# A two-layer encoder on one core: first-layer tokens grouped by residue modulo 16, and the third group's probabilities turned by VectorE

## The chip, the cores and the metric

The kernel runs on one core of one Trainium2 chip. A core has five engines, each with an instruction queue of its own: TensorE (PE; its weight loads are listed apart as PEld), VectorE (DVE), ScalarE (ACT), GpSimd (POOL) and SyncE (SP, which here only issues DMA transfers). PE writes its products to PSUM, in banks of 512 floats per partition; everything else lies in SBUF, 128 partitions wide, or in DRAM. The metric is the device time of one execution in microseconds. The kernel before takes 941.91 us, the median of three runs (941.63 to 941.92).

## The reference

An encoder of two layers on 512 tokens of 1024 features. The first layer's mixer is attention in three groups per head, and this is the part that the change touches; the second layer uses grouped-query attention over all tokens. Every layer has memory attention (4 heads, 256 memory tokens), a SiLU gate and an output projection.

```python
A_GROUPS = ((128, 1), (512, 4), (2048, 16))      # (window, dilation)

def mixer_dilated(qkv, qn_g, kn_g, ang):         # qkv: 3 x 3 groups x 8 heads x 128
    ...
    q = apply_rope(rmsnorm(q), ang) * (HEAD_DIM ** -0.5)
    k = apply_rope(rmsnorm(k), ang)
    for g, (window, dilation) in enumerate(A_GROUPS):
        # token t attends to t + j*dilation, |j| <= window/(2*dilation)
        o_g, l_g = dilated_window_attention(q[:, :, g], k[:, :, g], v[:, :, g], window, dilation)
    w = softmax over the three groups of their log-sum-exps
    return sum over g of w_g * o_g

for i in range(2):
    h = rmsnorm(x, norm_g[i])
    proj = h @ w_in[i]                           # mixer heads, memory queries, gates
    ...
    y = concatenate([o_mix, o_mem]) * silu(gate)
    x = x + y @ w_out[i]
```

With 512 tokens, the second group joins tokens of one residue class modulo 4 (128 of them, all within its window's blocks of 128 up to a mask), and the third one tokens of one residue class modulo 16 (32 of them).

## The kernel before

**Weights and products.** The weights (1024 rows, four bytes a number) stream from DRAM in transfers of 512 KB, issued by SP and in part by GpSimd (L261). Each large product is made from seven products of sums of blocks (named "12", "11", "S1", "S2", "S4", "S3", "22"; of both factors). For precision each factor is a rounded high part and a low part, its remainder: the weights' high part is cast by ScalarE (L323), the low part is subtracted by DVE (L333), and PE takes three products of parts, L176, L177 and, for the weights' low parts, L180. The partial results in PSUM (pool `pj`, four banks) are copied out by ScalarE (L398) or added onto a tile `sn` by DVE (L420). Transposes, scores and attention products use a second pool of four banks (`at`).

**Tokens.** Chunk c (0 to 3) of the first layer holds the tokens 4p+c, p = 0 to 127 on the partitions. The transposed rows of x have the chunks side by side, p along the free dimension; products of the projection again have p on the partitions. One chunk is thus a residue class modulo 4: the second group attends inside a chunk, and the third one inside the tokens with equal p modulo 4 of a chunk. `first_t` and `diffs_t` transpose the normed rows on PE into a PSUM bank and read them from there; `setup` loads the mask and the rotary table `tabA` with p on the partitions, and the weights `grA` of the norms.

**One head** (`head_chunk`, then `attn_a`). A chunk of the projection gives q, k and v of the three groups for one head. After norm and rotation q and k are transposed (L641); `put` (L1255 to L1263) copies them: `qs`, `ks` for groups two and three with columns in order of the chunk, and `qk0` for the first group with columns in token order, written with a step of four floats. v of groups two and three stays in place (`v12`). v of the first group, of all heads, was computed before and stored in DRAM in token order (`v0d`, by `ev_v0`, L1183, eight transfers).

In `attn_a`, o = 0 is the first group, with probabilities of 128 tokens by 256 neighbours; o = 1 the second and the third together, 128 by 2 x 128 per chunk. The scores (L1298, L1302) get the mask and their maximum on DVE (L1308) and the exponential on ScalarE (L1280). The statistics (maximum and sum) are swapped between the two orders of tokens through DRAM: tile `ds`, stored by L1336 and L1337, loaded back by L1339 and L1340 (SP). From them come factors for each token, by which `scale` (L1376, head 7 L1374) multiplies the probabilities. `turn(1)` transposes eight 128x128 blocks on PE (L1389) into two banks, the first copied by ScalarE, the second by DVE (L1393, `copy`); k = 0 is the second group, k = 1 the third. `turn(0)` does the same for the first group. `pv` multiplies by v (L1410 for o = 1), and `comb` adds the first group's result to that of the others (L1422). The head's output, 128 features by 512 tokens in order of the chunks, goes to DRAM (`od`), but for head 7.

**The gates** (`gates`, used for both layers). Three chunks "m", "a" and "b" project the gates, transposed (features on the partitions, tokens along the free dimension). Each result gets tanh (ScalarE) and (1 + tanh) times itself (DVE); then `times` multiplies by the head's output, loaded back as `og` from `od` (L862) or, where a head's output is still in SBUF, one head at a time (L866). What comes out, `y` in high and low parts (L890, L892) or sums of it, is the moving factor of the output projection, whose result is added to x and goes to the second layer with tokens p on the partitions.

**Order.** The schedule is written out by hand. A driver hands out slots: between groups of PE's matmuls it runs one step of each generator; each `yield n` waits n slots; `drv.late`, `drv.soon` and `drv.spawn` put work into queues for later slots. Chunks of the first layer run in the order "01234567mab": while PE multiplies for chunk h, attention of head h-1 is interleaved, so heads 6 and 7 fall beside the gate chunks. Each engine runs its own queue strictly in that order.

## Time and profile before

| | before |
|---|---|
| time, median of 3 runs | 941.91 us (941.63 to 941.92) |
| the profiled execution: its time | 942.24 us |
| the profiled execution: span of the trace | 940.5 us |
| granted clock of TensorE over the span | 1.00 |
| HBM read, written | 158.31 MB, 11.08 MB |

The span runs from the first recorded instruction to the last; the execution's own time has 1.7 us around it. Rows give, for a group of instructions, the line of the kernel, the engine, the operation, the tile written and those read, shapes and count, then busy time, the mean of one in ns, and the idle time of that engine just before them with what ended it. The costliest groups:

```profile
L333 DVE TENSOR_TENSOR wo<-wl,wh 128x1024 fp32r<-128x1024 f32 x258 | 316.4, 1232 | 7.0 <-ACT wh L323 6.8
L323 ACT CAST wh<-wl 128x1024 fp32r<-128x1024 f32 x258 | 271.7, 1060 | 29.7 <-PE pj L177 15.6
L176 PE MATMUL pj<-wh,hS 128*128 128x512 f32 (+1 forms) x416 | 154.3, 380 | 0.0
```

The low parts of the weights take 316.4 us of DVE, the high parts 271.7 us of ScalarE.

### The profile page before, as it was taken

The page shows a single profiled execution, that of the slowest core. Times are in us where ns is not written, and L with a number is a line of the kernel's source. Part 1 is how long each engine was busy: PE and PEld are TensorE (multiplying, and loading weights), DVE is VectorE, ACT ScalarE, POOL GpSimd, SP SyncE. Part 2 cuts the span into 40 slices and gives each one's busy share as a digit, 9 for nine tenths or more (in the row PEclk, how much of TensorE's full clock was granted, in tenths as well). Part 3 has the DMA queues.
Part 4 walks back from the last instruction along what each step waited for, and adds up shares of the span by engine and source line. Part 5 has one row for each costly group of instructions (what it writes and reads, how often), then busy time and mean ns, then how long its engine had stood idle before and what let it go on. Part 6 is the DMA issues. An engine that isn't in the chain of part 4 may idle for free.

```text
span 940.5 us, 16300 instructions
## 1 busy us (share of the span) xinstructions
PE 932.8 (99%) x5500; PEld 819.9 (87%) x5500; DVE 798.6 (85%) x1442; ACT 691.3 (74%) x1720; POOL 346.0 (37%) x494
## 2 busy tenths in 40 slices
PE   8999999999999999999999999999999999999998
PEld 6889888888888888888889998888988999999886
DVE  6898676879888888889788899977998998689977
ACT  7775788677768686867675667637878887789774
POOL 3411425455554545463836111114262440111123
PEclk9999999999999999999999999999999999999999
DMA  9999937869787878696867889979985686785777
GB/s 355 386 259 336 299 91 190 278 139 256 158 250 147 260 154 268 158 268 136 249 165 206 246 200 243 305 229 326 270 203 122 166 239 168 199 221 126 190 173 179
DMA packets 89429, 207.15 MB, mean 220 GB/s; under 512 B 25217, under 2 KB 34689, under 8 KB 89346
## 3 DMA queue, kind: packets, MB, share of 16 engines
q1 hardware_dynamic: 68818, 140.64, 43.4%
q0 software_dynamic: 19520, 63.97, 36.9%
q10 hardware_dynamic: 1008, 1.51, 0.4%
q8 instruction: 43, 0.70, 0.3%
q14 instruction: 40, 0.33, 0.1%
HBM read 158.31 MB, written 11.08 MB: 180 GB/s over the span
## 4 chain that ended last, share of the span: by engine, by line
PE 91%; DVE 4%; DMA 3%; ACT 1%; issue 0%; SPq 0%; DVEq 0%; ACTq 0%
PE pj L176 24%; PE pj L177 24%; PE pj L180 23%; PE qT L641 2%; DMA og<-od 2%; PE ptb L1616 1%; PE sa L1302 1%; PE oo L1410 1%; PE pt L1389 1%; DMA wl<-in_wall_dram 1%; PE xT L536 1%; PE sa L1298 1%; DVE wo L333 1%; PE ob L180 1%; PE ob L177 1%; PE ob L176 1%
## 5 line engine op out<-in xcount | busy, mean ns | idle before, releaser
L333 DVE TENSOR_TENSOR wo<-wl,wh 128x1024 fp32r<-128x1024 f32 x258 | 316.4, 1232 | 7.0 <-ACT wh L323 6.8
L323 ACT CAST wh<-wl 128x1024 fp32r<-128x1024 f32 x258 | 271.7, 1060 | 29.7 <-PE pj L177 15.6
L176 PE MATMUL pj<-wh,hS 128*128 128x512 f32 (+1 forms) x416 | 154.3, 380 | 0.0
L177 PE MATMUL pj<-wh,hS 128*128 128x512 f32 (+1 forms) x416 | 148.9, 367 | 0.0
L176 PE MATMUL pj<-wh,h 128*128 128x512 f32 (+1 forms) x312 | 115.2, 378 | 0.0
L177 PE MATMUL pj<-wh,h 128*128 128x512 f32 (+1 forms) x312 | 111.7, 367 | 0.0
L484 POOL TENSOR_TENSOR rstd<-mse,half 128x4 f32<-128x4 f32 (+2 forms) x98 | 103.0, 1051 | 8.2
L180 PE MATMUL pj<-wo,hS 128*128 128x512 f32 (+1 forms) x416 | 99.5, 366 | 0.0
L177 PEld LDWEIGHTS pj<-wh,hS 128*128 128x128 f32 x416 | 78.7, 189 | 11.3
L176 PEld LDWEIGHTS pj<-wh,hS 128*128 128x128 f32 x416 | 78.6, 189 | 11.1 <-DVE sn L420 0.2
L483 POOL TENSOR_SCALAR mse<-hss 128x4 f32<-128x4 f32 (+1 forms) x88 | 46.1, 524 | 103.2 <-ACT junk L629 95.5
L180 PEld LDWEIGHTS pj<-wo,hS 128*128 128x128 f32 x416 | 72.4, 189 | 13.1
L629 ACT ACTIVATE junk<-sn 128x128 f32<-128x128 f32 x264 | 79.3, 311 | 2.2 <-DVE sn L411 2.1
L1246 POOL TENSOR_TENSOR ta<-sn,tabs 128x128 f32<-128x128 f32 (+1 forms) x64 | 35.9, 567 | 120.1 <-DVE sn L634 92.8
L398 ACT COPY sn<-pj 128x512 f32<-128x512 f32 x122 | 67.2, 590 | 16.6 <-PE pj L180 15.8
L180 PE MATMUL pj<-wo,h 128*128 128x512 f32 (+1 forms) x312 | 74.5, 365 | 0.0
L307 POOL DMA_DIRECT2D wl<-wl x34 | 30.2, 898 | 114.8 <-DVE wo L333 74.6
L261 POOL DMA_DIRECT2D wl<-in_wall_dram x40 | 38.1, 968 | 81.6 <-DMA wl<-in_wall_dram 35.3
L420 DVE TENSOR_TENSOR sn<-pj,sn 128x512 f32<-128x512 f32 x89 | 60.8, 684 | 7.1 <-PE pj L180 6.6
L177 PEld LDWEIGHTS pj<-wh,h 128*128 128x128 f32 x312 | 59.0, 189 | 8.4
L176 PEld LDWEIGHTS pj<-wh,h 128*128 128x128 f32 x312 | 59.0, 189 | 8.2
L180 PEld LDWEIGHTS pj<-wo,h 128*128 128x128 f32 x312 | 54.3, 189 | 9.7
(283 smaller groups left out, 2366.7 us busy)
## 6 DMA issues: line engine op xcount, KB each, us to landing
wl<-in_wall_dram SPq DMA_DIRECT2D x224, 512.0 KB, 7.5
wl<-wl POOLq DMA_DIRECT2D x68, 512.0 KB, 5.5
wl<-in_wall_dram POOLq DMA_DIRECT2D x44, 512.0 KB, 8.3
od<-o SPq DMA_DIRECT2D x11, 256.0 KB, 5.1
og<-od SPq DMA_DIRECT2D x10, 256.0 KB, 9.8
x<-in_x_dram SPq DMA_DIRECT2D x4, 512.0 KB, 9.0
v0d<-sn SPq DMA_DIRECT2D x8, 256.0 KB, 10.5
acc<-in_x_dram POOLq DMA_DIRECT2D x8, 256.0 KB, 7.1
```

The source lines that it names most:

```text
L176: T.matmul(o, a, b, start=start, stop=False, skip_group_check=True)
L177: T.matmul(o, c, d, start=False, stop=False, skip_group_check=True)
L180: T.matmul(o, a, b, start=False, stop=stop, skip_group_check=True)
L261: queue.dma_start(t, wall[d], **how)
L323: A.copy(wh, self.tile[self.items[i]])
L333: V.tensor_tensor(wo, self.tile[key], wh.bitcast(F32), ALU.subtract)
L398: A.copy(t, b)
L420: V.tensor_tensor(t, b, t, ALU.subtract if q == "12" else ALU.add)
L483: G.tensor_scalar(e, ss, EPS, None, ALU.add)
L484: G.tensor_tensor(r, e, half[:, 0:n], ALU.pow)
L629: A.activation(jk, p[:, j * 128:(j + 1) * 128], AF.Square, scale=by, accum_out=ss[:, j:j + 1])
L1246: G.tensor_tensor(ta[:, 0:n], xn[:, 0:n, 0:32], ropeA[:, 0, b, s0:s0 + n], ALU.mult)
```

## The change

Inside each chunk of the first layer the tokens get another order: column i*32 + a holds p = 4a + i (i = 0 to 3, a = 0 to 31), so that a residue class modulo 16 is a block of 32 columns. The order is made where the transposed rows of x are read from PSUM (`from_rows` on the read side, `by_class` on the written side); the products of the projection then have it on their partitions. The third group's probabilities of a chunk are now zero outside four diagonal blocks of 32x32, so the transpose of the 128x128 tile is that of its 32x32 blocks, and one `V.transpose` for the head takes the place of four PE transposes and of DVE's copy of their bank. The rest follows the order: the mask's half for groups two and three and the rotary table are loaded with the partitions in the new order (the mask through a tile `ok` and two GpSimd copies that also reorder its columns), v of the first group is stored in four transfers of 32 partitions instead of one, the copies into `qk0` write with a step of 16 floats instead of 4, `comb` reads with that step, the statistics' tile `ds` is laid out with the owner outermost, and the gates of the first layer (`perm=True`) write their product back in order of p, with a step of four floats, where their second tile `th` takes it in chunk "b". The second layer's calls are unchanged (`same`).

```diff
+    def by_class(t):
+        return t.rearrange("p k (i a) -> p k i a", i=4)
-    def first_t(H, top, c):
-        ps = [(k, turn4(top[j], *slot(H, k, c))) for k, j in (("12", 1), ("11", 0))]
-        for k, p in ps:
-            A.copy(whole(k, c), p)
+    def first_t(H, top, c, view=same, turn=same):
+        ps = [(k, turn(turn4(top[j], None, None)), [view(t) for t in slot(H, k, c)]) for k, j in (("12", 1), ("11", 0))]
+        for k, p, hl in ps:
+            split(*hl, p)
+        for k, p, _ in ps:
+            A.copy(view(whole(k, c)), p)
...
-    def gates(od, o_done, o_here, direct, forms=False):
+    def gates(od, o_done, o_here, direct, forms=False, perm=False):
...
+                def cls(t):
+                    return t.rearrange("p (m i a) -> p m i a", i=4, a=32) if perm else t
+                def rws(t):
+                    return t.rearrange("p (m a i) -> p m i a", i=4, a=32) if perm else t
...
-                        V.tensor_tensor(dst, t, got["o"], ALU.mult)
+                        V.tensor_tensor(rws(dst), cls(t), cls(got["o"]), ALU.mult)
...
-                            V.tensor_tensor(dv[:, n], tv[:, n], got[h][:, n], ALU.mult)
+                            V.tensor_tensor(rws(dv[:, n]), cls(tv[:, n]), cls(got[h][:, n]), ALU.mult)
...
-                times(t)
+                y = th if perm else t
+                times(y)
...
+    def from_rows(p):
+        return p.rearrange("p k (a i) -> p k i a", i=4)
...
     def setup():
-        nc.sync.dma_start(mask, mask_d)
-        nc.sync.dma_start(tabA, tab_a.rearrange("p (b c d) -> p b c d", b=2, c=4))
+        nc.sync.dma_start(mask[:, 0:256], mask_d[:, 0:256])
+        ok = s2(name="ok")[:, 0:256]
+        nc.sync.dma_start(ok, mask_d[:, 256:512].rearrange("(a i) k -> i a k", i=4))
+        nc.sync.dma_start(tabA.rearrange("p b c d -> p (b c d)"), tab_a.rearrange("(a i) f -> i a f", i=4))
...
+        for g in range(2):
+            G.tensor_copy(mask[:, 256 + g * 128:384 + g * 128].rearrange("p (i a) -> p i a", i=4), ok[:, g * 128:(g + 1) * 128].rearrange("p (a i) -> p i a", i=4))
...
-    v0w = v0d.rearrange("(p c) d -> c p d", c=4)
+    v0w = v0d.rearrange("(a i c) d -> c i a d", i=4, c=4)
...
-        nc.sync.dma_start(v0w[2 * i + u][:, j * 512:(j + 1) * 512], t)
+        for c in range(4):
+            nc.sync.dma_start(v0w[2 * i + u][c, :, j * 512:(j + 1) * 512], t[32 * c:32 * c + 32])
...
-                    A.copy(qk0[:, 0].rearrange("p (a c) -> p c a", c=4)[:, b], p[:, 0])
-                    V.tensor_scalar(qk0[:, 1].rearrange("p (a c) -> p c a", c=4)[:, b], p[:, 3], gk[:, 0:1], None, ALU.mult)
+                    q0, k0 = [qk0[:, n].rearrange("p (a i c) -> p c i a", i=4, c=4)[:, b] for n in range(2)]
+                    A.copy(q0, p[:, 0].rearrange("p (i a) -> p i a", i=4))
+                    V.tensor_scalar(k0, p[:, 3].rearrange("p (i a) -> p i a", i=4), gk[:, 0:1], None, ALU.mult)
...
-        ds = dram.tile([S, 2, 2], F32, name="ds")
-        nat_v = ds.rearrange("(b p) o s -> p b o s", b=4)
-        str_v = ds.rearrange("(p b) o s -> p b o s", b=4)
+        ds = dram.tile([2, S, 2], F32, name="ds")
+        nat_v = ds.rearrange("o (b p) s -> o p b s", b=4)
+        str_v = ds.rearrange("o (a i b) s -> o i a (b s)", i=4, b=4)
...
-                parts = [[(b, k) for b in range(4)] for k in range(2)]
+                parts = [[(b, 0) for b in range(4)]]
+                drv.late(lambda: V.transpose(pts[1][:, 1].rearrange("p (b q) -> p b q", b=4), prob[1][:, :, 128:256]))
...
-                        (V.tensor_copy if i else A.copy)(pts[o][:, i], pt)
+                        A.copy(pts[o][:, 0], pt)
...
-                    V.tensor_tensor(rs.rearrange("p (b a) -> p b a", b=4), oo.rearrange("p (a b) -> p b a", b=4),
-                                    rs.rearrange("p (b a) -> p b a", b=4), ALU.add)
+                    rv = rs.rearrange("p (b i a) -> p b i a", b=4, i=4)
+                    V.tensor_tensor(rv, oo.rearrange("p (a i b) -> p b i a", b=4, i=4), rv, ALU.add)
```

More of the change, by code (lines that the diff above doesn't have):

```diff
@@ L581, in slot, with same, diffs_t @@
         return part[k][:, 0, :, cs], part[k][:, 1, :, cs]
-    def first_t(H, top, c):
-        ps = [(k, turn4(top[j], *slot(H, k, c))) for k, j in (("12", 1), ("11", 0))]
-        for k, p in ps:
-            A.copy(whole(k, c), p)
-    def diffs_t(H, low, c):
+    def same(t):
+        return t
+    def by_class(t):
[6 more added lines that the diff above has]
+            A.copy(view(whole(k, c)), p)
+    def diffs_t(H, low, c, view=same, turn=same):
         f22 = whole("22", c)
-        A.copy(f22, turn4(low[1], None, None))
-        p = turn4(low[0], None, None)
+        A.copy(view(f22), turn(turn4(low[1], None, None)))
+        p = turn(turn4(low[0], None, None))
         yield 1
         s1, s3 = whole("S1", c), whole("S3", c)
-        V.tensor_tensor(s1, p, f22, ALU.subtract)
-        V.tensor_tensor(s3, full["11", c], p, ALU.subtract)
+        V.tensor_tensor(view(s1), p, view(f22), ALU.subtract)
+        V.tensor_tensor(view(s3), view(full["11", c]), p, ALU.subtract)
         split(*slot(H, "S1", c), s1)
@@ L889, in ev @@
                     return
-                A.copy(yt[j][0][:, :, ts], tv)
+                A.copy(yt[j][0][:, :, ts], yv)
                 yield 1
-                V.tensor_tensor(yt[j][1][:, :, ts], tv, yt[j][0][:, :, ts].bitcast(F32), ALU.subtract)
+                V.tensor_tensor(yt[j][1][:, :, ts], yv, yt[j][0][:, :, ts].bitcast(F32), ALU.subtract)
                 y_done.add((g, i, j))
@@ L1082, in prep @@
             if 1 < c < 4:
-                first_t(H, xb[c - 2], c - 2)
+                first_t(H, xb[c - 2], c - 2, by_class, from_rows)
             yield 1
         def forms(c):
-            yield from diffs_t(H, xb[2 + c], c)
+            yield from diffs_t(H, xb[2 + c], c, by_class, from_rows)
             yield 3
@@ L1335, in attn_a @@
         yield 1
-        nc.sync.dma_start(nat_v[:, :, 0, :], stp[:, 0])
-        nc.sync.dma_start(str_v[:, :, 1, :], stp[:, 1])
+        nc.sync.dma_start(nat_v[0], stp[:, 0])
+        nc.sync.dma_start(str_v[1], stp[:, 1].rearrange("p b s -> p (b s)"))
         yield Y[3]
-        nc.sync.dma_start(oth[:, 0], nat_v[:, :, 1, :])
-        nc.sync.dma_start(oth[:, 1], str_v[:, :, 0, :])
+        nc.sync.dma_start(oth[:, 0], nat_v[1])
+        nc.sync.dma_start(oth[:, 1].rearrange("p b s -> p (b s)"), str_v[0])
         yield Y[4]
@@ L1438, in attn_a @@
         put_od(h, rs)
-    gate, prep_y, YW, ys = gates(od, o_done, o_here, DIRECT)
+    gate, prep_y, YW, ys = gates(od, o_done, o_here, DIRECT, perm=True)
     for c in A_ORDER:
```

1 line of the change is left out of this document (added).

## The prediction

> **What bounds the kernel now.** I read the page's first part and its chain, then the busy time by stages, the chain in order of time, the timelines of VectorE and SP, and the groups that keep shapes apart.
>
> ```profile
> span 940.5 us, 16300 instructions
> PE 932.8 (99%) x5500; PEld 819.9 (87%) x5500; DVE 798.6 (85%) x1442; ACT 691.3 (74%) x1720; POOL 346.0 (37%) x494
> ...
> PE 91%; DVE 4%; DMA 3%; ACT 1%; issue 0%; SPq 0%; DVEq 0%; ACTq 0%
> ```
>
> TensorE (PE) carries 91% of the chain that ended last; 7% lie on VectorE (DVE) and DMA, and where these lie decides this case. Busy time by stages, columns span, PE, PEld, DVE, ACT, POOL, clock, DMA share, GB/s:
>
> ```profile
> 246.09:295.52 49.43, 49.43 (x262) 41.92 (x262) 41.82 (x95) 35.98 (x109) 26.27 (x40) 1.00 0.80 204
> 530.00:582.00 52.00, 51.73 (x368) 48.19 (x366) 51.61 (x96) 35.38 (x66) 6.06 (x7) 1.00 0.85 217
> ```
>
> The first row is one head chunk: PE full, DVE with 7.6 us to spare. In the second, around the gate chunks, DVE is busy 51.61 of 52.00 us: two engines are full at once. The chain there:
>
> ```profile
> 497.72 4.61 DMA ds<-stp
> 502.35 0.37 SPq L1339
> 502.81 0.81 SPq L1340
> 503.68 12.10 DMA wl<-in_wall_dram
> 515.85 14.12 DMA og<-od
> ...
> 538.26 1.00 DVE p L1376 x4
> ...
> 539.39 0.96 PE pt L1389 x7
> ...
> 581.30 0.87 PE pt L1389 x8
> ```
>
> So the og load that lands at 530.0 starts DVE, and DVE, not PE, then arrives last. What PE waits for between 525 and 612 us (in all, times, longest), and DVE's timeline:
>
> ```profile
> PEld pt L1389 <- issue: 0.5, 1, 0.5
> PEld pj L176 <- ACT acc L398: 0.4, 1, 0.4
> ```
> ```profile
> 530.00 0.69 DVE L862 TENSOR_TENSOR yf<-sn,og 128x512 f32<-128x512 f32 x1 [2.77 <-DMA og<-od]
> ...
> 580.60 0.68 DVE L862 TENSOR_TENSOR sn<-sn,og 128x512 f32<-128x512 f32 x1
> 581.21 1.28 DVE L420 TENSOR_TENSOR acc<-pj,acc 128x512 f32<-128x512 f32 x2
> ```
> ```profile
> 572.71 0.22 ACT L1350 ACTIVATE e<-d 128x16 f32<-128x16 f32 x1 [4.59 <-DVE d L1348]
> ```
> ```profile
> 581.95 0.51 PE L176 MATMUL pj<-wh,yS 128*128 128x512 f32 x1
> ```
>
> PE touches DVE three times here: at 539 (head 6's transposes wait for its scaling), at 575 (PE waits 0.4 us for ScalarE's copy of a bank, which is queued behind an exponential that waited for DVE), and at 582, where the fourth product of the output projection adds onto the bank that L420 has just read. The first of the two L420 ends near 581.85, the matmul begins at 581.95: 0.1 us of slack. From 530 to 582 DVE's queue is thus a second critical path.
>
> **The change, part by part.**
>
> *Removed on PE.* Of third-group transposes, four per head go, 32 in all. Eight take 0.87 us (row 581.30), so a head saves 0.435. Heads 0 to 5 turn before the og wait, in PE-bound chunks: 6 x 0.435 = **-2.61 us**. Heads 6 and 7 turn just before the meetings at 539 and 582, where PE would only wait longer: 0 for them. What is late next in the chunks is still PE; DVE's 7.6 us cover the rest.
>
> *The copy of the second transposed bank becomes V.transpose, at the same place in DVE's queue.* The transposition has no row. What it replaces is L1393, the last row here (the shape, count, busy time and mean ns of one, idle time before); the others serve the next parts:
>
> ```profile
> L1262 DVE TENSOR_SCALAR qk<-qT,gk 128x128 f32<-128x128 f32 x32 | 14.5, 453 | 13.0 <-ACT qk L1261 12.8 <-issue 0.3
> ...
> L1261 ACT COPY qk<-qT 128x128 f32<-128x128 f32 x32 | 12.8, 401 | 0.0
> ...
> L1260 ACT COPY qs<-qT 128x256 f32<-128x256 f32 x32 | 11.9, 372 | 30.2 <-PE qT L641 30.2
> ...
> L1258 DVE TENSOR_SCALAR ks<-qT,gk 128x128 f32<-128x128 f32 x32 | 10.5, 348 | 17.8 <-ACT ks L1257 17.7
> ...
> L1422 DVE TENSOR_TENSOR o<-oo,o 128x512 f32<-128x512 f32 x8 | 5.5, 691 | 18.5 <-PE oo L172 18.5
> L1393 DVE COPY pT<-pt 128x512 f32<-128x512 f32 x8 | 5.5, 687 | 0.0
> ```
>
> Bounds: 0.35 us (half the copy) and 1.37 (twice). I take the copy's own 0.69: **0**. Only head 6's lies in the full stretch ahead of 582, so this is at most -0.3 or +0.7.
>
> *The gates' multiplication now writes with a step of 16 bytes (tokens back in row order).* L1262 and L1258 are the same operation on 128 elements; L1262 alone writes with that step, and takes 453 against 348 ns: 0.82 ns more per element. ScalarE shows it too: L1261 takes longer for 128 stepped elements than L1260 for 256 dense ones. For 512 elements that is 0.42 us. Between 530 and 581.2 there are eight:
>
> ```profile
> L862 DVE TENSOR_TENSOR yf<-sn,og 128x512 f32<-128x512 f32 x6 | 4.1, 685 | 2.8 <-DMA og<-od 2.8
> ...
> L862 DVE TENSOR_TENSOR sn<-sn,og 128x512 f32<-128x512 f32 x2 | 1.4, 683 | 0.0
> ```
>
> Eight by 0.42 is 3.36, less the 0.1 of slack at 582: **+3.26 us**. Queued behind each are the weights' low parts, the scalings and the bank reads that PE meets. Bounds: 0 a piece if a two-operand write hides the step, 0.6 if reading beside it makes it half as dear again. The two earlier ones end inside the 2.77 us of idle before 530, so 0; without that cover, 0.84.
>
> *The four last multiplications (L866)* grow by 0.21 each, 0.84:
>
> ```profile
> 604.38 1.23 DVE L333 TENSOR_TENSOR wo<-wl,wh 128x1024 fp32r<-128x1024 f32 x1 [1.71 <-ACT wh L323]
> ...
> 608.07 1.29 DVE L892 TENSOR_TENSOR y<-sn,y 128x512 fp32r<-128x512 f32 x2
> ...
> 609.61 0.87 PEld L180 LDWEIGHTS pj<-wh,y 128*128 128x128 f32 x4
> ```
>
> DVE is tied to PE again here (the 1.71 us wait on ScalarE's cast). The low part ends at 609.36; PE needs the later heads' half at its third load, about 610.05: 0.7 us of slack, so **+0.1**.
>
> *Reads of PSUM with a step.* The combining add L1422 already reads its bank so, at 691 ns like a plain one, so I take 0 for DVE. Its step grows from 16 to 64 bytes (one add in the full stretch): 0 to 0.42. ScalarE's ten stepped reads at the start have no row: 0 to the price of a stepped write, 0.5 each, covered by its idle time there; I take 0. The writes of q and k go from a 16 to a 64-byte step; already one line each, I take 0 and up to 0.1 each, under the chunks' cover.
>
> *Statistics through DRAM.* The strided store and load merge four 8-byte pieces into one of 32. SP issues such loads (L1340) in 0.81 us against 0.37 (L1339), and the chain to og passes both: I take half the difference, **-0.2** (0 to -0.9, if the store's 4.61 us shrink by the whole of it as well).
>
> The Trainium skill, "DMA: Bandwidth & Descriptors", section "Why a DMA increments its semaphore by 16 and not by 1", speaks against this: a DMA is spread over the largest number up to 16 that divides both sides' slowest dimension, so the new views, whose slowest dimension is 4, would use 4 engines. No row here shows a view of that kind. By it the statistics gain nothing (128 pieces on 4 engines are as many each as 512 on 16), and the sum rises by 0.2.
>
> *v0 is stored in four pieces, 24 more DMAs on SP; the mask in two; two GpSimd copies.*
>
> ```profile
> 53.70 0.92 SPq L1183 DMA_DIRECT2D v0d<-sn  x2
> ...
> 56.23 0.41 SPq L1098 DMA_DIRECT2D grA<-in_qn_a_dram  x1
> ```
> ```profile
> v0d<-sn SPq DMA_DIRECT2D x8, 256.0 KB, 10.5
> ```
> ```profile
> SPq L261 <- DMA v0d<-sn: 3.1, 4, 2.2
> ```
> ```profile
> 69.96 0.20 DVE L1105 TENSOR_SCALAR grA<-grA 128x96 f32<-128x96 f32 x1
> ...
> 71.28 3.48 DVE L333 TENSOR_TENSOR wo<-wl,wh 128x1024 fp32r<-128x1024 f32 x3
> ```
> ```profile
> 78.33 0.96 PE pj L180 x8
> ```
> ```profile
> DMA to landing us min/median/max: 11.0/11.7/12.3
> ```
> ```profile
> 73.98 0.88 POOL L307 DMA_DIRECT2D wl<-wl  x1 [9.99 <-DVE wo L333]
> ```
>
> In order: SP's issues, the stores' median landing, a wait of SP, DVE's timeline, PE's chain, grA's landings, GpSimd's timeline. SP's weight loads wait for v0 stores to land: by the order of issues, the ninth DMA waits for the first. Eight pieces fill that depth. The two grA loads become the thirteenth and fourteenth and wait for the fifth and sixth piece, so they go out when the first whole store landed until now, 53.7 + 10.5 = 64.2, some 7 us later than 56.2 to 56.7. The weights behind them are as late; by the order of loads and casts each is asked for several products ahead of its cast, and that hides it: 0, and up to 7 us without that cover. GpSimd's two copies, at the 0.88 us of the nearest row each, fit its 9.99 us of idle: 0. What grA's lateness does is the rival below.
>
> **Sum**, against the profiled execution of 942.24 us (span 940.5 and 1.7 around it): -2.61 - 0.2 + 3.26 + 0.1 = +0.55, so 942.8. That execution lies 0.33 above the median of the runs shown, 941.91; the forecast for the median is **942.5**. Its own range, with 0.3 to 0.45 us per gate write and the small bounds, is 940.6 to 943.7.
>
> **Rivals.**
>
> *The stepped writes are cheap for a two-operand instruction, or og lands earlier* (the idle 2.77 us shrink). For: PSUM's stepped reads cost nothing. Against: both engines pay for such writes. At 0 to 0.1 us each: -2.61 - 0.2 + (0 to 0.8), the median at 939.1 to 939.9.
>
> *Slower: DVE stalls in setup.* L1105 sits in DVE's queue at 69.96 and needs grA, now landed at 67 to 69 (11.0 to 12.3 after the issue). Issued 7 us later and as slow, it lands at 74 to 76, and every weight part behind it waits. The first of the three parts from 71.28 is ready near 72.4, and PE's group that uses it (by count of parts and groups) starts at 78.3, 5.9 us on; so it decides from a landing after 75.9. Landings of 77.4 to 79.3, with further queueing, cost PE 1.5 to 3.4 us, the median at 944.0 to 945.9. Against: fewer bytes are queued ahead by then, so it may land sooner. By the skill's rule above, the mask and table loads on 4 engines would put it later still.
>
> *Slower: a dear transposition (+0.7), the 64-byte step (+0.4) and 0.5 us per write (+0.6)* together: 944.2.
>
> *The PE time does not go*, since another wait fills it in the chunks: the median 945.1 at most; no wait of PE in a chunk is near, so I fold it into the last one.
>
> **How the numbers follow.** Forecast 0.55, cheap writes 0.25, setup stall 0.12, dear operations 0.08. A measurement tells about 0.2%, 1.9 us, from no change, so 940.0 to 943.8 counts as the same. So faster 0.25, same 0.55, slower 0.20. The range for 8 in 10, 939.0 to 944.6, takes in the cheap writes and half of the slower cases.
>
> **What would show it.** L1389 with 96 matmuls, and chunks of 49.0 instead of 49.43 us; L862 of layer 1 at 1.1 us against 0.68; the wait before head 6's transposes grown from 0.5 towards 2 us, and more wait at 575 and 582; og landing near 527. Wrong would be L862 at 0.7 us, an og wait that vanishes, DVE idle before L1105, or chunks no shorter.

## The result and the profile after

The changed kernel takes 947.86 us (median of six runs, 946.75 to 948.78), the kernel before 941.77 us beside it (941.0 to 942.73). The ratio is 1.0064, with a 95% interval from 1.0051 to 1.0077: slower, by 6.1 us. The profiled execution has a span of 946.5 us against 940.5. From the page of the changed kernel, its first part and its chain:

```profile
span 946.5 us, 16275 instructions
PE 931.2 (98%) x5468; PEld 817.1 (86%) x5468; DVE 801.1 (85%) x1442; ACT 691.3 (73%) x1720; POOL 349.2 (37%) x496
...
PE 84%; DMA 6%; DVE 6%; ACT 2%; issue 1%; SPq 0%; POOL 0%; DVEq 0%; ACTq 0%; POOLq 0%
```

PE has 32 matmuls and 1.6 us less to do, as meant, but carries 84% of the chain instead of 91%. To see where it waits, follow one and the same instruction through both traces. The groups of L180 matmuls (each ends a product) are the same in both kernels:

| starts before at | starts after at | after is later by |
|---|---|---|
| 72.63 | 72.16 | -0.5 us |
| 75.35 | 77.16 | 1.8 us |
| 86.81 | 88.98 | 2.2 us |
| 104.61 | 113.22 | 8.6 us |
| 240.04 | 248.23 | 8.2 us |
| 289.49 | 297.24 | 7.8 us |
| 487.21 | 493.25 | 6.0 us |
| 537.88 | 543.49 | 5.6 us |
| 542.98 | 548.12 | 5.1 us |
| 577.49 | 583.28 | 5.8 us |
| 583.91 | 590.04 | 6.1 us |

Such a table is the quickest way to split a result: 9.1 us are lost between 72 and 113 us, 3.5 won back between 113 and 548, and 1.0 lost between 548 and 590. What follows keeps the distance. Its zero is not exact: at 72.63 us, ahead of the first stall, the runs below lie between -0.6 and +0.9 us (but for v0_act, which has lost time by then), and ds_alone, whose code is that of the kernel before up to there, at +0.4. So losses are read as differences between two rows. PE's longest waits in the changed kernel:

```profile
PE qT L1239 <- DVE sn L644: 4.7, 1, 4.7
...
PE pj L180 <- DVE wo L333: 2.1, 1, 2.1
```

**The head chunks** did what was forecast. One of them by stages, with the columns of the prediction's rows:

```profile
248.23:297.24 49.01, 49.01 (x258) 41.51 (x257) 41.59 (x95) 36.00 (x110) 26.26 (x40) 1.00 0.76 205
```

It is 0.42 us shorter than 49.43, with four matmuls fewer in the row. Groups that keep shapes apart, for the operations that had no row before:

```profile
L1290 DVE TENSOR_SCALAR qk<-qT,gk 128x128 f32<-128x128 f32 x32 | 14.2, 445 | 11.5 <-ACT qk L1289 11.5
...
L1418 PE MATMUL pt<-ident,p 128*128 128x128 f32 x96 | 13.1, 273 | 0.0
...
L1411 DVE STREAM_TRANSPOSE pT<-p 128x512 f32<-128x512 f32 x8 | 5.5, 692 | 0.0
L1452 DVE TENSOR_TENSOR o<-oo,o 128x512 f32<-128x512 f32 x8 | 5.5, 690 | 18.6 <-PE oo L172 18.6
```

VectorE's block transposition costs 692 ns where the copy cost 687. The combining add reads PSUM with 64 bytes of step at 690 ns (691 before), and the write with 64 bytes takes 445 ns (453 with 16).

**The first stall.** SP's issues, VectorE's timeline and the chain of the changed kernel:

```profile
53.40 4.00 SPq L1210 DMA_DIRECT2D v0d<-sn  x8
...
62.64 0.39 SPq L1122 DMA_DIRECT2D grA<-in_qn_a_dram  x1
```
```profile
74.56 0.21 DVE L1131 TENSOR_SCALAR grA<-grA 128x96 f32<-128x96 f32 x1 [3.26 <-DMA grA<-in_qn_a_dram]
...
75.89 3.48 DVE L333 TENSOR_TENSOR wo<-wl,wh 128x1024 fp32r<-128x1024 f32 x3
```
```profile
62.64 11.90 DMA grA<-in_qn_a_dram
...
75.97 1.14 DVE wo L333
77.16 1.20 PE pj L180 x4
```

grA goes out 6.4 us later than before (56.23) and lands at 74.5. VectorE stands 3.26 us for it, and the weights' low parts that begin at 75.89 instead of 71.28 reach PE too late: 2.3 us are lost by 77.16, 2.6 by 88.98.

The late issue is not the whole of it. The trace also keeps the time of every landing event that a transfer leaves at its semaphore, and most transfers leave sixteen. The load of the rotary table `tabA`, issued just ahead of grA, left sixteen in the kernel before; with its new view it leaves four, and so does `ok`. Fifteen of grA's sixteen had come by 67.95 us, and VectorE reached L1131 at 71.3. The sixteenth came at 74.54, 0.19 us behind the last of `tabA`'s four (74.35). So grA's place behind the table's load held it up as well; no run here separates the two.

**The second stall** is longer. Its links, again in the chain:

```profile
91.01 5.40 DMA v0d<-sn
...
96.92 0.58 ACT sn L398
97.50 0.87 ACT wh L323
98.37 6.19 DMA wl<-in_wall_dram
...
105.21 0.94 POOL wl L261
...
107.47 1.06 POOL rstd L484
108.55 0.70 DVE sn L644
...
109.30 0.85 PE qT L1239 x4
```

PE's timeline shows what the wait costs:

```profile
109.30 0.85 PE L1239 MATMUL qT<-ident,sn 128*128 128x128 f32 x4 [4.65 <-DVE sn L644]
...
110.37 0.63 PE L177 MATMUL pj<-wh,h 128*128 128x512 f32 x1
...
114.38 0.39 PE L177 MATMUL pj<-wh,h 128*128 128x512 f32 x1
```

The wait of 4.65 us is not all of the 6.4 that the table shows here. Behind it the granted clock of TensorE is 0.66 from 109 to 111 us and 0.50 from 111 to 113, and a matmul of 128x512 takes 0.63 us instead of 0.39. The transposes and the eight matmuls behind them take 3.9 us (109.30 to 113.22) where they took 2.3 before (102.32 to 104.61): another 1.6 us.

A weight load, issued at 98.37, lands at 104.56. GpSimd's next instruction is L261, which adds a second block of weights to it by an accumulating transfer; it can't start before. Behind it in GpSimd's queue stands the norm step L484, behind that VectorE's multiplication, behind that PE's transposes. GpSimd's timeline before and after shows one wait that grew:

```profile
97.32 1.87 POOL L261 DMA_DIRECT2D wl<-in_wall_dram  x2 [7.99 <-DMA wl<-in_wall_dram]
```
```profile
105.21 1.87 POOL L261 DMA_DIRECT2D wl<-in_wall_dram  x2 [11.93 <-DMA wl<-in_wall_dram]
```

The load is late because of what SP does ahead of it. Before, the weight loads went out from 84.03; now:

```profile
84.03 28.24 SPq L261 DMA_DIRECT2D wl<-in_wall_dram  x10
```
```profile
83.15 5.83 SPq L1210 DMA_DIRECT2D v0d<-sn  x8
89.09 1.10 SPq L261 DMA_DIRECT2D wl<-in_wall_dram  x1
90.29 4.90 SPq L1210 DMA_DIRECT2D v0d<-sn  x4
95.30 0.44 SPq L261 DMA_DIRECT2D wl<-in_wall_dram  x1
95.84 2.44 SPq L1210 DMA_DIRECT2D v0d<-sn  x4
98.37 17.66 SPq L261 DMA_DIRECT2D wl<-in_wall_dram  x9
```

Sixteen pieces of v0 pass in 15 us: four pieces take SP from 2.4 to 4.9 us, where one store was one issue of 0.32. They hold more than SP's queue: by the chain, a piece issued at 91.01 lands at 96.41, ScalarE's copy L398 into a result tile and its next cast stand behind that landing, and the load goes out when that cast ends, 0.1 us after SP has got rid of its last pieces.

**The gate chunks.** VectorE's timeline at the place of the old og wait (the third of these multiplications, at 530.00 before), then the gates' multiplication between 525 and 617 us by groups:

```profile
532.32 1.22 DVE L333 TENSOR_TENSOR wo<-wl,wh 128x1024 fp32r<-128x1024 f32 x1
533.46 1.10 DVE L878 TENSOR_TENSOR yf<-sn,og 128x512 f32<-128x512 f32 x1
```
```profile
L878 DVE TENSOR_TENSOR yf<-sn,og 128x512 f32<-128x512 f32 x7 | 7.7, 1102 | 0.0
```

The multiplication takes 1.10 us instead of 0.685, the forecast 0.42 more. But the idle 2.77 us before it are gone, since og is there in time.

### The profile page after: what moved, and what is told of

Its sections match the earlier page's. It is cut to its first block, busy times and chain, and to the rows that moved or that the text cites. A ratio compares the mean times of both kernels' runs of the same rounds, so it can differ in the third digit from the quotient of the medians.

```text
span 946.5 us, 16275 instructions
## 1 busy us (share of the span) xinstructions
PE 931.2 (98%) x5468; PEld 817.1 (86%) x5468; DVE 801.1 (85%) x1442; ACT 691.3 (73%) x1720; POOL 349.2 (37%) x496
## 4 chain that ended last, share of the span: by engine, by line
PE 84%; DMA 6%; DVE 6%; ACT 2%; issue 1%; SPq 0%; POOL 0%; DVEq 0%; ACTq 0%; POOLq 0%
PE pj L176 22%; PE pj L177 22%; PE pj L180 22%; PE qT L651 2%; DVE wo L333 2%; DMA wl<-in_wall_dram 2%; PE sa L1330 2%; PE oo L1439 2%; PE ptb L1645 1%; PE sa L1326 1%; DMA grA<-in_qn_a_dram 1%; PE pt L1418 1%; DMA wl<-wl 1%; DMA x<-in_x_dram 1%; DMA row<-in_norm_g_dram 1%
## 5 line engine op out<-in xcount | busy, mean ns | idle before, releaser
L484 POOL TENSOR_TENSOR rstd<-mse,half 128x4 f32<-128x4 f32 (+2 forms) x98 | 103.6, 1057 | 8.2
L180 PE MATMUL pj<-wo,hS 128*128 128x512 f32 (+1 forms) x416 | 99.5, 366 | 0.0
L483 POOL TENSOR_SCALAR mse<-hss 128x4 f32<-128x4 f32 (+1 forms) x88 | 48.6, 553 | 101.1 <-ACT junk L639 93.2
L180 PEld LDWEIGHTS pj<-wo,hS 128*128 128x128 f32 x416 | 72.5, 189 | 13.2
L398 ACT COPY sn<-pj 128x512 f32<-128x512 f32 x122 | 67.1, 589 | 17.3 <-PE pj L180 17.3
L180 PE MATMUL pj<-wo,h 128*128 128x512 f32 (+1 forms) x312 | 74.7, 366 | 2.1 <-DVE wo L333 2.1
L261 POOL DMA_DIRECT2D wl<-in_wall_dram x40 | 38.0, 966 | 81.7 <-DMA wl<-in_wall_dram 41.4
L420 DVE TENSOR_TENSOR sn<-pj,sn 128x512 f32<-128x512 f32 x89 | 60.7, 683 | 5.8 <-PE pj L180 5.4
L180 PEld LDWEIGHTS pj<-wo,h 128*128 128x128 f32 x312 | 54.3, 189 | 12.3 <-DVE wo L333 2.5
```

Source lines behind the costliest of these rows:

```text
L180: T.matmul(o, a, b, start=False, stop=stop, skip_group_check=True)
L261: queue.dma_start(t, wall[d], **how)
L398: A.copy(t, b)
L420: V.tensor_tensor(t, b, t, ALU.subtract if q == "12" else ALU.add)
L483: G.tensor_scalar(e, ss, EPS, None, ALU.add)
L484: G.tensor_tensor(r, e, half[:, 0:n], ALU.pow)
```

## The experiments

All compare with the kernel before on the same chip: its median was 942.27 us beside v0_plain, v0_one, gr_first and ds_alone, 942.14 beside v0_act and the three kernels with other gates, 941.94 beside t3_late, both_late, pool_gates and pe_turn, 941.83 beside t3_eight and early_setup. "PE's offset" is the last column of the table above, for the kernel in question.

**Theory S:** the 32 pieces crowd SP's queue, which makes the loads behind them late. **Rival M:** the setup loads' new views and GpSimd's copies do it.

*v0_plain*

```diff
-    v0w = v0d.rearrange("(a i c) d -> c i a d", i=4, c=4)
+    v0p = v0d.rearrange("(p c) d -> c p d", c=4)
...
-        for c in range(4):
-            nc.sync.dma_start(v0w[2 * i + u][c, :, j * 512:(j + 1) * 512], t[32 * c:32 * c + 32])
+        nc.sync.dma_start(v0p[2 * i + u][:, j * 512:(j + 1) * 512], t)
```

> The changed kernel with each block of v0 stored by one plain transfer again (rows of v0 stay in the new order, so the first group meets the wrong values). Theory S, SyncE's queue: the 32 pieces fill it, so grA lands late (PE +2.2 us by 89 us) and later stores hold result tiles, ScalarE's copies, a weight load and GpSimd's accumulation (PE +6.4 us more at 109 us). Then both stalls go: PE's groups after 105 us come at most 1.5 us later than in the kernel before, and the time is 939.5 to 941.5 us. Rival M, the mask and the table: their new views and the two GpSimd copies make the delay; then the time stays at 946 to 948 us.

Measured 941.1 us, ratio 0.999 [0.9981, 0.9999]. PE's offset is 0.3 us at 240 instead of 8.2; both stalls are gone, with mask, table and copies as in the changed kernel. M alone falls. (The table's four landing events are the same here; its last comes at 67.86, and grA's at 68.03, in time.)

*v0_one*

```diff
-        for c in range(4):
-            nc.sync.dma_start(v0w[2 * i + u][c, :, j * 512:(j + 1) * 512], t[32 * c:32 * c + 32])
+        nc.sync.dma_start(v0w[2 * i + u][:, :, j * 512:(j + 1) * 512], t)
```

> The changed kernel with the same new order of v0's rows, but one transfer for each block whose DRAM side has i, a and the columns as dimensions. Theory S: what counts is the number of transfers in SyncE's queue; the time is as with the plain store, 939.5 to 941.5 us, and a block lands in about the 10.5 us of before. Rival E, few engines: a transfer whose slowest dimension is 4 goes over 4 engines, lands in over 15 us and holds its result tile so long that ScalarE's copy waits again; 943 to 948 us.

Measured 958.95 us, ratio 1.0176 [1.0162, 1.019]: worse than expected by either theory. The number of transfers isn't all. SP's issues in v0_one, then the busy time of 88 to 92 us in it and in the kernel before (the last two figures are the DMA share and GB/s):

```profile
62.40 9.31 SPq L1122 DMA_DIRECT2D grA<-in_qn_a_dram  x1
```
```profile
88.00:92.00 4.00, 4.00 (x36) 4.00 (x34) 4.00 (x5) 1.61 (x2) 0.00 (x0) 1.00 0.35 88
```
```profile
88.00:92.00 4.00, 4.00 (x36) 4.00 (x35) 1.88 (x4) 2.55 (x3) 1.25 (x2) 1.00 1.07 296
```

SP stands at grA for 9.31 us, behind the first two stores and the setup loads, and from 88 to 92 us the 16 DMA engines are busy to a share of 0.35 only, against 1.07 before. PE's offset at 104.61 is 18.6 us. So a store with a slowest dimension of 4 seems to let most engines idle: rival E, only dearer than it said. The Trainium skill, "DMA: Bandwidth & Descriptors", section "Why a DMA increments its semaphore by 16 and not by 1", which the prediction weighed for other transfers, says just this (4 of 16 engines); the share of 0.35 agrees. The landing events agree too: each of these stores leaves four behind the one at its issue, where a plain store of the kernel before leaves sixteen, and the last comes 9 to 17 us after the issue. A weight load issued behind them at 93.61 has twelve of its sixteen events by 97.18 and the other four between 108.78 and 110.94: the loads behind stand in line on the few engines that carry the stores.

*gr_first*

```diff
+        nc.sync.dma_start(grA[:, 0:3], qn_a[0:1, :, 0:32].to_broadcast([128, 3, 32]))
+        nc.sync.dma_start(grA[:, 3:6], kn_a[0:1, :, 0:32].to_broadcast([128, 3, 32]))
         nc.sync.dma_start(mask[:, 0:256], mask_d[:, 0:256])
...
-        nc.sync.dma_start(grA[:, 0:3], qn_a[0:1, :, 0:32].to_broadcast([128, 3, 32]))
-        nc.sync.dma_start(grA[:, 3:6], kn_a[0:1, :, 0:32].to_broadcast([128, 3, 32]))
```

> The changed kernel with the two grA loads issued ahead of mask, ok and table. If the first stall (PE +1.8 us at 77 us) is grA's lateness, L1131 starts before 73 us instead of 74.56 and that stall shrinks to below 0.5 us. The second stall has a cause of its own in SyncE's queue between 83 and 98 us: theory S says it takes back most of what the first gives, and the time is 946.5 to 947.9 us. If instead the second only carries on the first, the time is 943.5 to 946 us.

Measured 949.29 us, ratio 1.0072 [1.0058, 1.0086]. L1131 starts at 70.02 without a wait, PE's offset is 0.2 us at 86.81 (0.0 at 72.63): the first stall was grA's lateness. At 104.61 the offset is 9.4 us all the same, and PE's wait for L644 is 7.0 instead of 4.7 us. The second stall has a deadline of its own, and PE now only arrives earlier to wait for it. The time lies above the expected range: nothing is given back, and behind the longer wait the granted clock stays low for longer (0.73, 0.50, 0.50 and 0.56 in the four stretches of 2 us from 107 to 115).

*v0_act*

```diff
-            nc.sync.dma_start(v0w[2 * i + u][c, :, j * 512:(j + 1) * 512], t[32 * c:32 * c + 32])
+            nc.scalar.dma_start(v0w[2 * i + u][c, :, j * 512:(j + 1) * 512], t[32 * c:32 * c + 32])
```

> The changed kernel with all 32 pieces of v0 issued by ScalarE instead of SyncE. Theory S: SyncE's weight loads and setup loads go out as early as before (the load that GpSimd's sums wait for near 84 us instead of 98), both stalls go, and the time is 940.5 to 943 us. Rival: the pieces now hold ScalarE's queue, in which the weights' casts stand, for 0.4 us each or until an earlier piece lands; the stalls come back as late casts, 944 to 950 us.

Measured 953.16 us, ratio 1.0123 [1.0109, 1.0137]: the rival, above its range. ScalarE's timeline:

```profile
87.77 6.83 ACTq L1210 DMA_DIRECT2D v0d<-sn  x8
94.64 0.59 ACT L398 COPY sn<-pj 128x512 f32<-128x512 f32 x1 [9.39 <-DMA v0d<-sn]
```

The eight pieces stand in the queue that copies PSUM out, and PE waits for a free bank (6.9 us in all for L420 behind it). The pieces need a queue with nothing urgent in it. SP's and ScalarE's are not such queues; GpSimd's, in which the sums stand, wasn't tried.

**Theory Q:** the second stall is GpSimd's queue standing behind the late sums (T3), and not a lack of weights.

*t3_late* and *t3_eight*: the sums become due five, or eight, slots after their load.

```diff
                 elif k == "T3":
-                    if not self.ripe(self.load_at, key, force):
+                    if not self.ripe(self.load_at, key, force, 5 if c == 4 else None):
```

> The changed kernel, but GpSimd issues the two sums T3 of the first head's weights five slots after their load instead of two, so that two of its norm steps come ahead of them. Theory Q: the second stall (VectorE's and PE's wait near 105 to 109 us for L484's rstd) is GpSimd's queue standing behind a sum whose load SyncE issued late; then PE's wait of 4.7 us goes, the stall of 1.8 to 2.2 us for grA stays, and the time is 942.5 to 944.5 us. Rival: PE is short of weights there anyway; the wait moves to the casts and the time stays at 946 us or more.

Measured 942.03 us, ratio 1.0006 [0.9996, 1.0016]: 0.5 us below the expected range. PE's wait for L644 is 1.5 us instead of 4.7, its offset at 110.53 is 4.1 us.

> As t3_late, with eight slots instead of five between the T3 loads and their sums, so that four norm steps pass ahead. Theory Q: t3_late kept a stall of 1.5 us because two steps (of four) still stood behind the sums. Then PE's offset against the kernel before stays at about 2.3 us after 89 us, falls by 3.4 in the head chunks and rises by 1.0 in the gate chunks: 941.2 to 942.2 us. Rival: the sums, now later, make the casts of T3 late near 119 us, or PE loses elsewhere to SyncE's queue: 943 us or more.

Measured 941.52 us, ratio 0.9996 [0.9987, 1.0004]. PE's wait for L644 is gone; the offset is 1.3 us at 86.81 and 0.9 at 240. GpSimd's timeline shows what passes ahead of the sums now:

```profile
103.61 1.88 POOL L484 TENSOR_TENSOR rstd<-mse,half 128x4 f32<-128x4 f32 x1
...
108.40 1.04 POOL L484 TENSOR_TENSOR rstd<-mse,half 128x4 f32<-128x4 f32 x1
109.39 1.92 POOL L261 DMA_DIRECT2D wl<-in_wall_dram  x2
```

L261 no longer waits, and the norm steps don't wait for it. The T3 load still goes out as late, at 100.5 us; nothing on PE needs it so soon. That is theory Q.

*both_late*: t3_late and gr_first together.

> The same with grA's two loads also issued ahead of mask and table. By theory Q both stalls are gone and the whole change keeps its 3.4 us of PE less the loss in the gate chunks: 940.3 to 942.3 us, as with v0's plain store. Rival: another wait behind SyncE's 32 pieces takes their place: 943.5 us or more.

Measured 946.98 us, ratio 1.0046 [1.0032, 1.006]: a miss. Here SP issues the T3 load at 102.75, and five slots are too few again:

```profile
110.76 0.87 POOL L261 DMA_DIRECT2D wl<-in_wall_dram  x1 [9.09 <-DMA wl<-in_wall_dram]
```

PE waits 4.8 us for L644. The same mechanism, with a later deadline; the rival's "another wait" isn't it. The clock falls behind this wait too (0.80, then 0.50 to 119 us), and the offset reaches 8.0.

*early_setup*: t3_eight, with the setup loads ahead of v0's first pieces.

```diff
-BULK, ACTIVE, SET_AT, MEM_B, PREP_Y, PREP_B, HALF, SET_B = 2, 2, 15, 14, 1, 1, {"a": 3, "b": 3, "o": 0}, 12
+BULK, ACTIVE, SET_AT, MEM_B, PREP_Y, PREP_B, HALF, SET_B = 2, 2, 13, 14, 1, 1, {"a": 3, "b": 3, "o": 0}, 12
...
     def setup():
...
-        yield 4
+        yield 6
```

> t3_eight with the setup loads issued two slots earlier, ahead of v0's first eight pieces, and their use at its old place. Theory S: grA lands before L1131 needs it, the first stall goes too, and with both gone the change keeps what it saves: 939 to 940.5 us, below the kernel before. Rival: v0's pieces or the weight loads behind the setup loads come so much later that a stall returns: 942 us or more.

Measured 940.38 us, ratio 0.9986 [0.9977, 0.9995], the only version with nothing left out or misplaced whose interval lies below the kernel before. Its profiled execution isn't typical: 944.1 us, the slowest of eleven, with an offset of 4.3 us at 86.81, where VectorE waits 4.2 us for a weight load (L292). Nine of the eleven took 939.8 to 941.8 us. SP's queue is still full, and in this execution it showed.

**The gate chunks.** *steps_alone*: the kernel before with the stepped write alone.

```diff
-                        V.tensor_tensor(dst, t, got["o"], ALU.mult)
+                        V.tensor_tensor(rws(dst), cls(t), cls(got["o"]), ALU.mult)
...
-    gate, prep_y, YW, ys = gates(od, o_done, o_here, DIRECT)
+    gate, prep_y, YW, ys = gates(od, o_done, o_here, DIRECT, perm=True)
```

> The kernel before with the first layer's gates written as in the changed one, with a step of 16 bytes, nothing else (its tokens are misplaced by it). The prediction's term: eight writes of 1.1 instead of 0.68 us behind the late og make VectorE 3.3 us later at the output projection, and PE with it: 944.7 to 945.8 us. Rival: PE's own bound lies so far behind VectorE's queue that most is hidden: 942 to 943.5 us.

Measured 944.57 us, ratio 1.0023 [1.0014, 1.0032], just below the expected range; the span is 942.8, 2.3 us over the kernel before, of which 0.6 stood at 75.35 us already. PE's offset is 0.7 us at 487, 0.3 at 543 (the wait before head 6's transposes has gone here too) and 2.3 at 584. VectorE's timeline:

```profile
529.26 1.12 DVE L868 TENSOR_TENSOR yf<-sn,og 128x512 f32<-128x512 f32 x1 [0.72 <-DMA og<-od]
```

Of the 2.77 us of idle before it, 0.72 are left: the two earlier writes take 0.8 of them, and the rest, 1.2 us, is og's earlier landing in this execution.

*dense_gates*: the changed kernel without the step.

```diff
-    gate, prep_y, YW, ys = gates(od, o_done, o_here, DIRECT, perm=True)
+    gate, prep_y, YW, ys = gates(od, o_done, o_here, DIRECT)
```

> The changed kernel with the gates' multiplication left in the new order of columns and written densely (the token order isn't restored, so rows come out misplaced). Theory: the step costs PE 1.0 us in the gate chunks, since VectorE's idle time of 2.77 us before the first of eight multiplications is gone: 946.3 to 947.2 us. Rival: the 1.0 us is due to other things in these chunks (the stepped reads of the combining add, transfers): 947.6 us or more.

Measured 946.52 us, ratio 1.0047 [1.0034, 1.006]. Its offset at 240 us is 6.6 us against 8.2 in the trace of the changed kernel, with the same code in setup, so the time says little; the later offsets do. From 487 to 584 us the changed kernel's goes from 6.04 to 6.13, this one's from 4.47 to 2.75. The step costs PE 1.8 us in the gate chunks, more than the 1.0 that the expectation had read off the table, because without it PE would have won 1.7 there.

*ds_alone*: the kernel before with the statistics' layout alone.

```diff
-        ds = dram.tile([S, 2, 2], F32, name="ds")
-        nat_v = ds.rearrange("(b p) o s -> p b o s", b=4)
-        str_v = ds.rearrange("(p b) o s -> p b o s", b=4)
+        ds = dram.tile([2, S, 2], F32, name="ds")
+        nat_v = ds.rearrange("o (b p) s -> o p b s", b=4)
+        str_v = ds.rearrange("o (p b) s -> o p (b s)", b=4)
```

> The kernel before with the statistics' tile laid out by owner, nothing else. Theory: with fewer 8-byte pieces SyncE passes the loads of statistics and v 2 us sooner, og is issued near 513.7 instead of 515.85 us and VectorE's wait of 2.77 us before the gates' multiplication goes; PE then loses no more than 0.1 of its 0.5 and 0.4 us in the gate chunks: 940.7 to 941.3 us. Rival: og's lateness is not due to the statistics; the wait stays over 2 us and the time is 941.4 to 942 us.

Measured 941.9 us, ratio 0.9998 [0.9989, 1.0007]. VectorE's timeline:

```profile
526.53 1.22 DVE L333 TENSOR_TENSOR wo<-wl,wh 128x1024 fp32r<-128x1024 f32 x1
527.66 0.68 DVE L862 TENSOR_TENSOR yf<-sn,og 128x512 f32<-128x512 f32 x1
```

The og wait goes, as in the changed kernel, so it was very likely the statistics' layout that took it away there. (The views differ: here the slowest dimension stays 128, there it is 4, with four landing events. The strided load still lands sooner in both: its last event comes at the median 10.0 us after the end of its issue in the kernel before, 8.7 here, 8.6 in the changed kernel.) PE gains 0.9 us by it, as expected: its offset is 0.5 us at 487, 0.0 at 543 and -0.4 at 584, so the waits of 0.5 and 0.4 us are gone. The median is 0.4 us lower, which lies in the rival's range and can't be told from nothing. VectorE was not the only bound there: with the 2.8 us of its wait gone, PE is full.

*read_step*: the step moved from the write to both reads.

```diff
-                    return t.rearrange("p (m i a) -> p m i a", i=4, a=32) if perm else t
+                    return t.rearrange("p (m i a) -> p m a i", i=4, a=32) if perm else t
...
-                    return t.rearrange("p (m a i) -> p m i a", i=4, a=32) if perm else t
+                    return t.rearrange("p (m a i) -> p m a i", i=4, a=32) if perm else t
```

> The changed kernel with the gates' multiplication written densely and both factors read in token order, so with a step of 128 bytes. If only writes pay for a step, it takes 0.68 us again, PE's loss of 1.0 us in the gate chunks goes, and the time is 946.3 to 947.4 us. If reads pay too, at two stepped operands it takes 1.1 us or more, and the time is 947.8 us or more (up to 950 at 1.5 us).

Measured 949.01 us, ratio 1.0073 [1.006, 1.0086].

```profile
L878 DVE TENSOR_TENSOR yf<-sn,og 128x512 f32<-128x512 f32 x7 | 8.6, 1228 | 0.0
```

Two reads with 128 bytes of step cost 1.23 us, more than the write's 1.10. Reads pay too, as the second half of the expectation had it.

*pool_gates*: both_late with these multiplications on GpSimd.

```diff
-                        V.tensor_tensor(rws(dst), cls(t), cls(got["o"]), ALU.mult)
+                        (G if perm else V).tensor_tensor(rws(dst), cls(t), cls(got["o"]), ALU.mult)
```

> The kernel both_late with the first layer's eight to ten stepped gate multiplications (L878) done by GpSimd instead of VectorE. If VectorE's queue is what PE loses to in the gate chunks, the 1.8 us that the stepped writes cost there go: 938.5 to 940.5 us. Rival: GpSimd's queue stands behind its sums of weights (waits of up to 15 us), or slows VectorE beside it; the products come late and the time is 942 to 948 us.

Measured 946.04 us, ratio 1.0052 [1.0039, 1.0065]; both_late's second stall is in it. In the gate chunks PE's offset goes from 3.54 to 3.49 (487 to 584), both_late's from 5.48 to 5.57: 0.1 us won, not 1.8. Groups from 515 to 592 us:

```profile
L333 DVE TENSOR_TENSOR wo<-wl,wh 128x1024 fp32r<-128x1024 f32 x21 | 29.1, 1385 | 0.0
L878 POOL TENSOR_TENSOR yf<-sn,og 128x512 f32<-128x512 f32 x8 | 15.9, 1985 | 21.9 <-DVE sn L888 18.3 <-DMA og<-od 3.6
```

VectorE's weight parts take 1.385 us there instead of 1.213 in dense_gates; one GpSimd product took 5.75 us. These rows look as if the two engines hold each other up. The Trainium skill, "SBUF — State Buffer", section "SBUF: two separate sides", says that an operation of VectorE with two inputs from SBUF and one of GpSimd that reads SBUF exclude each other for their whole length; these rows agree, and 21 longer parts by 0.17 us give 3.6 us of VectorE back. That this ate the gain is argued, not shown: VectorE also waits 1.2 us for a product of GpSimd that comes late (L945).

*pe_turn*: both_late with the transposes on PE again.

```diff
-                parts = [[(b, 0) for b in range(4)]]
+                parts = [[(b, k) for b in range(4)] for k in range(2)]
...
-                drv.late(lambda: V.transpose(pts[1][:, 1].rearrange("p (b q) -> p b q", b=4), prob[1][:, :, 128:256]))
...
-                        A.copy(pts[o][:, 0], pt)
+                        (V.tensor_copy if i else A.copy)(pts[o][:, i], pt)
```

> The kernel both_late with the third group's transposes back on PE and VectorE's copy of their bank in place of its block transposition. Theory: each head chunk is 0.44 us longer (49.4 instead of 49.0), eight heads 3.0 to 3.5 us, so 2.6 to 3.5 us more than both_late. Rival: the chunks are bound by something else and the gain came from elsewhere: within 1 us of both_late.

Measured 949.0 us, ratio 1.0076 [1.0063, 1.0088], 2.0 us more than both_late. Chunks last 49.4 to 49.5 us again, and PE's offset stays at 6.8 from 113 to 487 us while both_late's falls from 8.0 to 5.5. The gain of the head chunks is the four transposes and nothing else. The 2.0 us of the medians lie below the expected 2.6 to 3.5; in the profiled executions pe_turn's offset was 1.2 us the smaller one when the second stall was over.

## Why the prediction was wrong

The forecast of 942.5 us stood on four terms and a zero. By the table of offsets the changed kernel's 6.0 us of span are:

- *Heads 0 to 5, -2.61.* Measured 8.61 to 6.04, so -2.57: right. pe_turn shows the cause.
- *Heads 6 and 7, 0, as PE would only wait longer.* For head 6, wrong in the good sense: the offset falls by 0.43 before 543 and by another 0.47 at 543, where the wait of 0.5 us for VectorE's scaling has gone. That wait hung on og (ds_alone wins the same 0.47 there). For head 7 the saving counts too: from 543 to 584 us dense_gates wins 0.8 us, ds_alone 0.4.
- *The gate writes, +3.26.* The price of one was right (1.10 against the 0.685 + 0.42 worked out from L1262 and L1258). The sum was too large: alone it costs 1.6 to 2.0 us by steps_alone's offsets and 2.4 by its median, in the changed kernel 1.8 (dense_gates, by offsets alone). What failed is the anchor: og's landing was taken as fixed relative to PE but for 0.2 us, and it moved by far more: in the changed kernel this load goes out 3.7 us later (519.51 instead of 515.85) while PE is 6.0 later, and og's landings take 6.7 us at the median instead of 9.8.
- *The four last multiplications, +0.1.* The offset stays at 6.1 us from 590 to the end: nothing to be seen.
- *The statistics, -0.2.* Mis-sized: the og wait of 2.77 us went whole (ds_alone), and alone that is worth 0.9 us to PE. The rest of the 2.77 pays only beside the stepped writes, as cover that they use up. The objection that four engines would take the gain away was not borne out: the strided load leaves four landing events and lands sooner all the same.
- *SP and setup, 0.* This is the step that failed. It stands in the sentence that the weights are as late, but "each is asked for several products ahead of its cast, and that hides it: 0, and up to 7 us without that cover". The cover was counted to the casts. The weights of T3 have an earlier user: the sum that GpSimd adds two slots after the load, in an instruction that blocks its queue, with norm steps behind it on which PE depends. Measured 9.1 us, from -0.5 to 8.6 in the table: 2.6 in the first stall, 6.4 here, of which 4.7 are PE's wait and 1.6 slower matmuls behind it.

The rival "DVE stalls in setup" named the right queue and the right load. It gave 1.5 to 3.4 us from a landing after 75.9; grA landed at 74.5 and cost PE 2.3 to 2.6 us, because the weight part that came late is used by the group at 75.35 in the trace before, not by that at 78.33. Its remark that the mask and table loads would put grA later still fits the landing events. But it followed only the first eight pieces, to the loads next behind them. The other 24, between 74 and 98 us, weren't followed to any load, and the larger stall lies there.

The gates and the statistics together come to +0.1 from 487 to 584 us with head 6 in it, against the forecast 3.1: two errors that nearly hid each other, and neither changed the sign. v0_plain shows what is left without the stalls: -1.2 us against the kernel before.

What stays open: why the setup stall varies between executions of the same code (PE's offset at 240 us was 8.2 us in the changed kernel, 6.6 in dense_gates, 6.5 in read_step), and how much of the time of four pieces in SP's queue is their landing and how much the weight loads that they share it with; and how much of grA's lateness is its late issue and how much its place behind the table's load. The stepped writes and the transposes weren't tried on a version with empty setup stalls, only by offsets.

## What to carry to other kernels

A transfer cut into pieces must be followed through its whole queue: list every load that is issued behind each piece, and for each its first user on every engine, sums and accumulations on GpSimd included, and then what stands behind that user in its queue. For a view with a new shape, count the landing events that its transfer leaves: where they are few, the loads behind it can be held up in part. An idle stretch ahead of a full engine is cover for exactly its own length; before an edit is costed against it, ask what else in the same change moves its two ends. To place a gain or loss, follow one instruction that both kernels have through both traces, and read the difference between two rows of the offset, not its distance from zero.

## What the runs showed of the hardware

- A VectorE transposition of four 128x128 fp32 tiles in 32x32 blocks costs as much as a copy of the same 128x512 elements: 692 and 687 ns.
- For 128x512 fp32 in SBUF, a product costs 0.685 us dense, 1.10 with its write stepped by 16 bytes, 1.23 with both reads stepped by 128 bytes. For 128 elements a step of 64 bytes is no dearer than one of 16 (445 and 453 ns). A read of PSUM with a step of 64 bytes costs VectorE no more than one of 16 (690 and 691 ns), and about what L420's dense read costs (683).
- A 256 KB store in one transfer with a slowest dimension of 4 left four landing events where a plain one left sixteen, and was worse for the queue than its four pieces: a span of 956.6 against 946.5 us, and 938.7 with plain stores.
- Behind PE's wait of 4.65 us the granted clock of TensorE fell to 0.50 and a 128x512 matmul took 0.63 us instead of 0.39. It also fell behind the waits of 2.2 us (read_step) and 2.7 us (dense_gates) at the same place, and stayed at 1.00 behind 1.5 us (t3_late).
